# Gate and up projections: seven block products in place of eight, over all tokens at once

## Chip, cores and metric

One core of a Trainium2 chip runs the kernel. The metric is the device time of one execution in microseconds (us), the median of three runs. TensorE is written PE, its weight load PEld, VectorE DVE, ScalarE ACT, GpSimd POOL; SP is the queue that issues most DMAs.

## The reference, cut to what matters

A decoder block over 1024 tokens of width 1024 in float32. What the change touches is the feed-forward part; the first half of the block (a combined input projection, a state-space and a retention group, an output projection) comes ahead of it.

```python
x = x + einsum("bse,ed->bsd", mixed, w_out)
h = rmsnorm(x, norm2_w)
a = silu(einsum("bsd,df->bsf", h, w_gate))     # w_gate: 1024 x 2816
u = einsum("bsd,df->bsf", h, w_up)             # w_up:   1024 x 2816
x = x + einsum("bsf,fd->bsd", a * u, w_down)   # w_down: 2816 x 1024
return rmsnorm(x, final_norm_w)
```

## The kernel before, in words

Every float32 operand of a large projection is split in two: a high part rounded to fp32r (by ACT) and the exact rest (by DVE), `split` at L190 and `divide` at L238. A product of two such operands is three matmuls: high x high, high x low, low x high (`three`, L251).

The tokens are worked on in two halves of 512. A `Block` (L214) is 512 columns of a weight for the tokens of one half. Its steps are the k tiles of the contraction: a step takes a 128-row tile of the weight through 4 output tiles x 3 matmuls of 128x512. All steps of all blocks stand in one list, `steps`, and `run_all` (L316) walks it: at step i it first divides the weights up to step i + 3 (`ahead`, L290), whose loads go out three steps before that on SP's queue (`advance`, L300), then issues the step's matmuls, then what hangs on the step by `at` (L205). Matmuls and transposes keep the order in which they are traced; for the other engines the framework's scheduler picks the order, by priority (weight divisions and evacuations are raised by `PRIO`) and by what is ready.

The order of blocks (L931 to L939) is: input projection of half 0 and of half 1, output projection of half 0 and of half 1, then for each half gate/up (`gate_up_block`, L840) and down (`down_block`, L868). A gate/up block takes 256 gate columns and the 256 up columns that belong to them, 8 steps; there are 11 for each half. Its four sums lie in four of the eight PSUM banks (`banks`, L284); when a sum is complete, `evac` (L850) forms tanh on ACT, multiplies twice on DVE and splits the result into `aT`, 22 pairs of tiles that stay in SBUF (slots m0 to m15, qk, ktok) until the down blocks of the same half have used them. A down block is 22 steps.

The norm ahead of gate/up is `norm_pieces` (L326): `scale` turns the sums of squares into factors and scales four tiles of x in place; eight pieces then transpose 128 channels each through PSUM and split them. The hooks at L1041 to L1048 place half 0's pieces under the output projection of half 1 and half 1's under the down projection of half 0. x after the output projection lies in slots x4 to x7 for half 0 and x0 to x3 for half 1, and is also kept in DRAM (`x2D`), from which the down block loads it again.

Of the kernel before, what the change touches and what calls it, by code (L numbers as in the profile page):

```python
# [29 lines left out]
NXB = 12           # channel tiles of the convolution  # L30

# columns of the constant array
_o = np.cumsum([0, 128, 128, 128, RH * 128, 8 * 32, 8 * 32, RH, RH, 4])
# [3 lines left out]
def _constants():  # L37
    f = np.float32
    c = np.zeros((P, K_N), f)
    i = np.arange(P)  # L40
    c[:, K_ID:K_ID + P] = np.eye(P)
# [16 lines left out]
    return c  # L58
# [6 lines left out]
def block_kernel(ctx: ExitStack, tc: tile.TileContext, x, norm1_w, w_in, conv_w, conv_b,  # L65
# [26 lines left out]
    # ------------------------------------------------------------------ constants  # L92
    kc = T([P, K_N], "kc")
    rows1 = T([8, P], "rows1")
    rows = T([84, P], "rows")
    nc.scalar.dma_start(kc[:, :K_TRI], consts[:, :K_TRI])
# [7 lines left out]
    ident = kc[:, K_ID:K_ID + P]  # L104
# [11 lines left out]
    def load_small():  # L116
        nc.sync.dma_start(kc[:, K_TRI:], consts[:, K_TRI:])
# [9 lines left out]
    # by channel: norm1, norm2, conv_w / 2, conv_b / 2, ret_norm_w / 2, ssd_norm_w  # L127
# [20 lines left out]
    x2D = [[dt_([P, DM], f"x2D{h}{c}") for c in range(NT)] for h in range(2)]  # L148

    # ------------------------------------------------------------------ helpers  # L150
# [5 lines left out]
    def mm(o, a, b, start=True, stop=True):  # L156
        tc.keep_in_program_order(nc.tensor.matmul(o, a, b, start=start, stop=stop))  # L157
# [7 lines left out]
    def rsqrt(dst, src, scale, eps, n):  # L165
        """dst = 1 / sqrt(src * scale + eps), on [P, n]."""
# [11 lines left out]
    def rsqrt1(dst, src, scale, eps):  # L178
        """the same on [P, 1]."""
# [10 lines left out]
    def split(pair, src):  # L190
        """pair[:, 0] = src rounded to fp32r, pair[:, 1] = the exact rest."""
        act(pair[:, 0], src, AF.Copy)
        tt(pair[:, 1], src, pair[:, 0].bitcast(F32), op=ALU.subtract)
# [131 lines left out]
    # ------------------------------------------------------------------ norms  # L325
    def norm_pieces(get, wcol, tags, res):  # L326
        """get() gives NT tiles [P, DM], scaled in place, and their sums of squares; res gets
        the pairs [ch, 2, tok] of what is normed and transposed."""
# [11 lines left out]
        def one(k):  # L340
            def f():
# [3 lines left out]
                hp = T([P, 2, TH], tags[k], F32R)  # L345
# [3 lines left out]
                res.append(hp)  # L349
            return f  # L350
# [89 lines left out]
    def qk_block(h, b):  # L440
        """b=0: dt and q heads 0-3; b=1: q heads 4-7, k heads 0-1; b=2: k heads 2-7."""
# [71 lines left out]
    # ------------------------------------------------------------------ ssd  # L513
# [23 lines left out]
    def cs_stage(h):  # L537
# [11 lines left out]
        ex = T([P, 4, n], "ex", bufs=2)      # a_cs, exp(a_cs), exp(suffix), exp(total)  # L549
# [5 lines left out]
    def hbc(a, c, g, n=SP_):  # L555
        """per head scalars of chunk c, group g, over the n columns of a head."""
# [14 lines left out]
    def ssd_pieces(h, W):  # L571
# [10 lines left out]
        def sz(c, g):  # L582
            def f():
                # 2 * silu(z) by channel; times y in place
# [7 lines left out]
        def s1(c, g):  # L592
            def f():
# [24 lines left out]
                if not first:  # L618
                    C = W([P, 8, P])         # C, decayed from the chunk's start, for each head
# [52 lines left out]
        def s3(c):  # L672
            def f():
                # sums of squares over a group's channels, by token
# [7 lines left out]
        # the first half's z of group 1 comes late  # L682
# [11 lines left out]
    # ------------------------------------------------------------------ retention  # L694
    def ret_pieces(h, W):
# [3 lines left out]
        def r1(c):  # L699
            def f():  # L700
# [9 lines left out]
                # even heads in the first bank, odd heads in the second: their q and k lie on  # L710
                # different halves of the partitions
# [81 lines left out]
    # ------------------------------------------------------------------ out-projection  # L793
    def out_blocks(h):
# [22 lines left out]
                    # the gate carries 2 * silu(z): so does the sum of squares, by 4  # L817
# [15 lines left out]
        # the ssd groups' norms scale their parts of the sum  # L833
# [5 lines left out]
    # ------------------------------------------------------------------ feed-forward  # L839
    def gate_up_block(h, b):  # L840
        d = H[h]

        def begin(blk):
            if b == 0:
                d["aT"] = [T([P, 2, TH], f"m{k}", F32R) for k in range(16)]
                q1 = T([P, 4, 2, TH], "qk", F32R)
                q2 = T([P, 2, 2, TH], "ktok", F32R)
                d["aT"] += [q1[:, k] for k in range(4)] + [q2[:, k] for k in range(2)]

            def evac(j, ps):  # L850
                if j < 2:
                    return
                f = 2 * b + j - 2
                g, u = ps[j - 2], ps[j]
                if j == 2:
                    t = T([P, 2, TH], "S")
                    t, a = t[:, 0, :], t[:, 1, :]
                else:
                    t, a = T([P, TH], "u", bufs=2), T([P, TH], "u", bufs=2)
                act(t, g, AF.Tanh, scale=0.5)  # L860
                stt(t, t, 1.0, g, op0=ALU.add, op1=ALU.mult)
                stt(a, u, 0.5, t, op0=ALU.mult, op1=ALU.mult)
                split(d["aT"][f], a)
            return evac
        return Block(True, lambda: d["hT2"], [(w_gate, 256 * b, 256), (w_up, 256 * b, 256)], begin,
                     pool=None)

    def down_block(h, b):  # L868
        d = H[h]

        def begin(blk):
# [15 lines left out]
            def evac(t, ps):  # L887
# [7 lines left out]
                # the end: no wait but for what the last products give  # L895
# [6 lines left out]
                # the mean square so far, and EPS  # L902
# [3 lines left out]
                if b == 1:  # L906
# [27 lines left out]
    for h in range(2):  # L934
        H[h]["O"] = list(out_blocks(h))
    for h in range(2):
        d = H[h]
        d["GU"] = [gate_up_block(h, b) for b in range(NF // 2)]
        d["D"] = [down_block(h, b) for b in range(2)]  # L939

    # first half's norm
# [66 lines left out]
    def late_small():  # L1008
        # not ahead of the first steps' work, on either engine
# [30 lines left out]

    for h in range(2):  # L1041
        d = H[h]
        d["hT2"] = []
# [38 lines left out]
```

## Time and profile before

| | |
|---|---|
| device time, median of 3 runs | 1579.66 us (1578.94 to 1580.57) |
| profiled execution: span, first to last instruction | 1577.9 us |
| its mean granted PE clock | 0.994 of full speed |
| PE busy | 1555.8 us, 99% |
| DVE busy | 901.3 us, 57% |
| ACT busy | 623.0 us, 39% |
| DMA | 206.65 MB, mean 131 GB/s |

The span is one profiled execution's; that execution's own time is taken as its span and the 1.8 us by which the median of the runs is longer. Busy shares are means over stages that differ. A line number in a row is one of the listing above; L157 is the helper that records every matmul and L160 the one for transposes, so there the tile names tell more: `wp` is a divided weight, `h` a normed activation, `m` a slot of many uses, L and M the two sets of PSUM banks.

### The profile page before, as it was taken

What the parts mean: (1) busy time and instruction counts of PE and PEld (TensorE: products, weight loads), DVE (VectorE), ACT (ScalarE), POOL (GpSimd) and SP (SyncE); (2) the same over time, 40 slices, a digit from 0 to 9 for tenths busy, and PEclk for the clock granted to TensorE, in tenths of its full rate; (3) what the DMA queues carried; (4) which work ended last, traced back from release to release, by engine and by line L of the source; (5) the groups of instructions that cost most, each with busy time, mean ns of one, the idle gap of its engine ahead of it and who ended that gap; (6) DMA issues with size and microseconds to landing.
All of it is one profiled execution on the core that took longest, in us unless ns stands there. A gap on an engine that the chain in (4) does not pass through costs nothing.

```text
span 1577.9 us, 21658 instructions
## 1 busy us (share of the span) xinstructions
PE 1555.8 (99%) x7672; PEld 1272.0 (81%) x7672; DVE 901.3 (57%) x1975; ACT 623.0 (39%) x1195; POOL 36.9 (2%) x67
## 2 busy tenths in 40 slices
PE   7999999999999999999999999999999999999997
PEld 5888878888898888787888888888888888888886
DVE  4477798567798984687544444343326344434244
ACT  5344457435446564244333333232323333323231
POOL 1012000000000000000000000000000000000000
PEclk8999999999999999999999999999999999999999
DMA  7433465554344577466343333333244333332231
GB/s 194 131 90 102 142 199 176 170 183 133 89 114 150 167 236 257 135 197 197 123 154 111 94 93 94 97 95 96 88 147 147 95 93 94 94 93 94 96 110 68
DMA packets 149933, 206.65 MB, mean 131 GB/s; under 512 B 14564, under 2 KB 91200, under 8 KB 149824
## 3 DMA queue, kind: packets, MB, share of 16 engines
q1 hardware_dynamic: 148656, 203.82, 42.2%
q0 software_dynamic: 432, 0.59, 0.6%
q8 instruction: 60, 0.98, 0.3%
q10 hardware_dynamic: 736, 0.86, 0.2%
q14 instruction: 49, 0.40, 0.1%
HBM read 175.78 MB, written 29.43 MB: 130 GB/s over the span
## 4 chain that ended last, share of the span: by engine, by line
PE 97%; DMA 2%; DVE 1%; ACT 1%; issue 0%; SPq 0%; ACTq 0%
PE L L157 77%; PE M L157 18%; PE M L160 2%; DMA wr<-in_w_in_dram 1%; DMA m<-mixD 0%; DMA kc<-in_consts_dram 0%; DMA x2D<-x 0%; DVE x L828 0%; DVE wp L245 0%; ACT x L435 0%; ACT wp L244 0%; ACT m L616 0%; DVE nw L187 0%; ACT u L196 0%; ACT m L806 0%
## 5 line engine op out<-in xcount | busy, mean ns | idle before, releaser
L245 DVE TENSOR_TENSOR wp<-wr,wp 128x512 fp32r<-128x512 f32 (+2 forms) x504 | 339.7, 674 | 571.1 <-ACT wp L244 444.0
L244 ACT ACTIVATE wp<-wr 128x512 fp32r<-128x512 f32 (+2 forms) x504 | 311.7, 619 | 757.5 <-PE L L157 546.2
L157 PE MATMUL L<-h,wp 128*128 128x512 f32 x2280 | 553.5, 396 | 0.0
L157 PEld LDWEIGHTS L<-h,wp 128*128 128x128 f32 x2280 | 425.8, 188 | 103.6 <-issue 1.0
L157 PE MATMUL L<-wp,m 128*128 128x512 f32 x1512 | 357.4, 395 | 0.3 <-DVE x L825 0.3
L157 PEld LDWEIGHTS L<-wp,m 128*128 128x128 f32 x1512 | 282.0, 188 | 65.8 <-DVE x L825 1.0
L157 PE MATMUL L<-wp,h 128*128 128x512 f32 (+2 forms) x1248 | 260.0, 365 | 0.0
L157 PEld LDWEIGHTS L<-wp,h 128*128 128x128 f32 x1248 | 215.3, 188 | 30.6 <-issue 5.1
L157 PE MATMUL M<-h,wp 128*128 128x512 f32 x792 | 198.9, 395 | 0.0
L157 PEld LDWEIGHTS M<-h,wp 128*128 128x128 f32 x792 | 148.5, 188 | 36.1
L378 DVE SCALAR_TENSOR_TENSOR m<-m,cols,m 128x512 f32<-128x512 f32 x72 | 52.1, 745 | 3.6 <-ACT m L376 3.4
L196 ACT ACTIVATE u<-x 128x512 f32<-128x512 f32 x48 | 29.9, 624 | 25.0 <-DVE x L889 19.5
L157 PE MATMUL L<-m,h 128*128 128x512 f32 x96 | 25.9, 421 | 10.7 <-ACT h L984 10.4
L157 PE MATMUL L<-wp,qk 128*128 128x512 f32 x144 | 34.5, 398 | 0.0
L616 ACT ACTIVATE m<-M,dtw 128x64 f32<-128x64 f32 x128 | 29.9, 328 | 11.4 <-DVE m L613 11.3
L806 ACT ACTIVATE m<-m,cols 128x512 fp32r<-128x512 f32 x32 | 22.7, 721 | 27.1 <-DMA m<-mixD 26.8
L157 PEld LDWEIGHTS L<-wp,qk 128*128 128x128 f32 x144 | 27.0, 188 | 6.4
L157 PEld LDWEIGHTS L<-m,h 128*128 128x128 f32 x96 | 18.7, 201 | 16.3 <-ACT h L984 11.7
L157 PE MATMUL M<-m,m 128*64 128x128 f32 (+1 forms) x288 | 30.8, 278 | 0.0
L160 PEld LDWEIGHTS M<-kc,x 128*128 128x128 f32 x192 | 24.3, 145 | 6.8 <-issue 1.8
L160 PE MATMUL M<-kc,x 128*128 128x128 f32 x192 | 29.4, 280 | 0.0
L623 DVE TENSOR_SCALAR m<-m,ex 128x128 f32<-128x128 f32 x128 | 27.9, 279 | 0.1
(213 smaller groups left out, 1163.6 us busy)
## 6 DMA issues: line engine op xcount, KB each, us to landing
wr<-in_w_in_dram SPq DMA_DIRECT2D x144, 256.0 KB, 2.8
wr<-in_w_gate_dram SPq DMA_DIRECT2D x176, 128.0 KB, 2.1
wr<-in_w_up_dram SPq DMA_DIRECT2D x176, 128.0 KB, 2.2
wr<-in_w_down_dram SPq DMA_DIRECT2D x88, 256.0 KB, 2.6
wr<-in_w_out_dram SPq DMA_DIRECT2D x64, 256.0 KB, 3.0
x<-in_x_dram SPq DMA_DIRECT2D x16, 512.0 KB, 4.4
m<-rD SPq DMA_DIRECT2D x16, 512.0 KB, 4.3
m<-mixD SPq DMA_DIRECT2D x32, 256.0 KB, 4.2
```

Of the source, the lines that this page charges most:

```text
L157: tc.keep_in_program_order(nc.tensor.matmul(o, a, b, start=start, stop=stop))
L160: tc.keep_in_program_order(nc.tensor.transpose(o, a, ident))
L196: act(T([P, 512], "u", bufs=2)[:, :src.shape[-1]], src, AF.Square, accum_out=dst)
L244: newest["act"] = act(pair[:, 0, :n], raw[:, :n], AF.Copy).ins
L245: newest["dve"] = tt(pair[:, 1, :n], raw[:, :n], pair[:, 0, :n].bitcast(F32), op=ALU.subtract).ins
L378: stt(dst, u[:, q:q + TH], w[q], dst, op0=ALU.mult, op1=ALU.add)
L616: act(xdte[:, hs], xp[:, hs], AF.Copy, scale=d["dte"][:, r0 + q:r0 + q + 1])
L623: ts(E[:, q, :], E[:, q, :], ex[:, 0, r0 + q:r0 + q + 1], 0.0, op0=ALU.subtract, op1=ALU.min)
L806: act(pair[:, 0], raw, AF.Copy, scale=w)
```

## The change

Gate and up are no longer done for one half of the tokens after the other. A `Unit` is 256 columns of one weight (gate or up) for all 1024 tokens. The weight is cut in four blocks (512 rows of the contraction x 128 columns), the normed activations too (512 channels x 512 tokens), and Strassen's scheme in Winograd's form gives the four blocks of the result by seven block products. A block product is one step: 4 k tiles x 3 matmuls of 128x512. The sums of weight blocks are formed on DVE for each unit (`divide`), the sums of activation blocks once, ahead (`b_first`, `b_sums`, `b_rest`). The products gather in three banks per unit, X, Y and Z; what a bank holds between two products is copied or added out (`c1`, `u2`, `c15`).

The order is now: both output projections, all of gate/up, down of half 0, down of half 1. Since the block sums need both halves normed, half 1's norm follows its output projection at once; the first eight steps of gate/up are products 1 and 2 of the first four units, which need half 0 alone. The other five products of these four units come next, then 18 units of seven. The gated result goes to DRAM (`aD`), and each down projection loads it again and splits it under its first block. Slots change hands: x0 to x3 take the whole weights (1 MB per unit, two loads), x4 to x7 join the divided weights' slots, and the constants' tile is used for sums (the identity moves to a tile of its own). Comments in the code are dropped; lines that only lose a comment are left out of the diff here.

```diff
@@ norm_pieces @@
-    def norm_pieces(get, wcol, tags, res):
+    def norm_pieces(get, wcol, tags, res, also=None):
...
-                hp = T([P, 2, TH], tags[k], F32R)
+                if also and k < 4:
+                    if k == 0:
+                        st["qk"] = T([P, 4, 2, TH], "qk", F32R)
+                    hp = st["qk"][:, k]
+                else:
+                    hp = T([P, 2, TH], tags[k], F32R)
...
                 res.append(hp)
+                if also:
+                    also(k)(b, w)
@@ feed-forward @@
-    def gate_up_block(h, b):
...
+    def b_first(k):
+        def f(b, w):
+            if k < 4:
+                B["F"].append(T([P, 2, TH], f"h{k}" if k < 3 else "S"))
+            act(B["F"][k % 4][:, k // 4, :], b, AF.Copy, scale=w)
+        return f
+
+    def b_sums(k):
+        def f():
...
+            for q in (k + 4, k):
+                b = bank("M")
+                for t in range(NT):
+                    tr(b[:, t * P:(t + 1) * P], H[1]["x2"][t][:, q * P:(q + 1) * P])
+                bs.append(b)
+            t2, t1 = bs
+            b22 = T([P, TH], "u", bufs=2)
+            act(b22, bs[0], AF.Copy, scale=cols[:, 12 + k:13 + k])
+            F = B["F"][k]
+            stt(t1, bs[1], cols[:, 8 + k:9 + k], F[:, 0], op0=ALU.mult, op1=ALU.subtract)
+            tt(t2, b22, t1, op=ALU.subtract)
+            split(B[6][k], t2)
+            split(B[5][k], t1)
+            tt(F, F, t2.unsqueeze(1).to_broadcast([P, 2, TH]), op=ALU.subtract)
+            split(B[3][k], b22)
+        return f
+
+    def b_rest(k):
+        def f():
+            split(B[7][k], B["F"][k][:, 0])
+            B[4].append(T([P, 2, TH], f"h{(k + 3) % 4}", F32R))
+            split(B[4][k], B["F"][k][:, 1])
+        return f
+
+    slots = [("wp", 3), ("x4", 1), ("wp", 3), ("x5", 1), ("wp", 3), ("x6", 1), ("x7", 1)]
...
+    class Unit:
...
+        ORDER = (1, 6, 5, 2, 7, 3, 4)
...
+        def load(self, k):
+            src = self.w[:, self.c0:self.c0 + 256].rearrange("(q k p) c -> q p k c", q=2, p=P)
+            if self.prods == (1, 2):
+                a = T([P, 4, P], "wr", bufs=5)
+                nc.sync.dma_start(a, src[k][:, :, :P])
...
+            elif k == 0:
+                u = self.parity = units[0] % 2
+                units[0] += 1
+                self.raw = [T([P, 4, 256], f"x{2 * u + q}") for q in range(2)]
+                for q in range(2):
+                    nc.sync.dma_start(self.raw[q], src[q])
+
+        def divide(self, k):
...
+                f = {1: A11, 2: A12, 4: A22}.get(i)
+            if i == 6:
+                f, op["s1"] = stage["s2"], T([P, 4, P], "wr", bufs=5)
+                tt(op["s1"], A21, A22, op=ALU.add)
+                tt(f, op["s1"], A11, op=ALU.subtract)
+            elif i == 5:
+                f = op.pop("s1")
+            elif f is None:
+                f = T([P, 4, P], "wr", bufs=5)
+                tt(f, *((A21, A11) if i == 7 else (A12, stage["s2"])), op=ALU.subtract)
+            op[i] = slot()
+            newest["act"], newest["dve"] = split(op[i], f)
+
+        def run(self, k):
+            i, st = self.prods[k], self.st
+            name = "XXYZYZZ"[i - 1]
+            if i in (1, 5, 6):
+                st[name] = next(any_bank)
+            ps, p = st[name], self.op.pop(i)
+            for q in range(4):
+                b = B[i][q]
+                st_ = i in (1, 5, 6) and q == 0
+                mm(ps, p[:, 0, q], b[:, 0, :], st_, False, skip_group_check=True)
+                mm(ps, p[:, 0, q], b[:, 1, :], False, False, skip_group_check=True)
+                mm(ps, p[:, 1, q], b[:, 0, :], False, q == 3, skip_group_check=True)
+            with tc.high_priority(PRIO):
+                if i == 1:
+                    copy(st["c1"], ps)
+                elif i == 6:
+                    st["u2"] = T([P, TH], "RS")
+                    tt(st["u2"], ps, st["c1"], op=ALU.add)
+                elif i == 5:
+                    st["c15"] = stage["c15"][:, self.parity]
+                    tt(st["c15"], ps, st["c1"], op=ALU.add)
+                else:
+                    q, add = {2: (0, None), 7: (3, "c15"), 3: (1, "u2"), 4: (2, "c1")}[i]
+                    self.use(q, ps, st[add] if add else None)
...
+            def gate(q, ps, add):
...
+                    tt(g, ps, add, op=ALU.add)
+                t = temp()
+                act(t, g, AF.Tanh, scale=0.5)
+                stt(ss[q], t, 1.0, g, op0=ALU.add, op1=ALU.mult)
+
+            def up(q, ps, add):
...
+                    tt(u, ps, add, op=ALU.add)
+                a = T([P, TH], "u", bufs=2)
+                stt(a, u, 0.5, ss[q], op0=ALU.mult, op1=ALU.mult)
+                nc.sync.dma_start(aD[q % 2][2 * b + q // 2], a)
...
+        EARLY = 4
+        us += [Unit(*a, (1, 2)) for a in todo[:EARLY]]
+        us += [Unit(*a, (6, 5, 7, 3, 4)) for a in todo[:EARLY]]
+        us += [Unit(*a) for a in todo[EARLY:]]
@@ down_block @@
+        def fetch(k):
...
+            nc.sync.dma_start(a[k][:, 1].bitcast(F32), aD[h][k])
+
+        def extra(k):
+            pair = d["aT"][k]
+            split(pair, pair[:, 1].bitcast(F32))
...
+                     (fetch, extra) if b == 0 else None,
@@ the program @@
+    s0 = H[1]["O"][0].first
+    at(s0 + 5, scale[0])
+    for k in range(8):
+        at(s0 + 9 + 2 * k, ks[0][k])
...
+    s0 = GU[0].first
+    at(s0 - 1, b_ready)
+    at(s0 - 1, scale[1])
+    for k in range(4):
+        at(s0 + 2 + k, b_sums(k))
+        at(s0 + 6, b_rest(k))
...
-    at(H[0]["GU"][2].first, load_final)
+    at(H[0]["D"][0].first, load_final)
```

## Rows read from the trace of the kernel before

**Rows 1.** Page: busy time, share of the span and instructions of each engine

```profile
PE 1555.8 (99%) x7672; PEld 1272.0 (81%) x7672; DVE 901.3 (57%) x1975; ACT 623.0 (39%) x1195; POOL 36.9 (2%) x67
```

**Rows 2.** Page: chain that ended last, shares by engine

```profile
PE 97%; DMA 2%; DVE 1%; ACT 1%; issue 0%; SPq 0%; ACTq 0%
```

**Rows 3.** Chain pieces (start, length, what); a window: engines, clock, DMA share, GB/s

```profile
961.10 23.10 PE L L157 x99
1005.90 23.10 PE L L157 x99
...
961.10:1005.90 44.80, 44.80 (x194) 35.90 (x193) 18.40 (x29) 14.81 (x24) 0.00 (x0) 1.00 0.32 94
```

**Rows 4.** Groups by line and form: busy us, mean ns | idle before

```profile
L245 DVE TENSOR_TENSOR wp<-wr,wp 128x512 fp32r<-128x512 f32 x456 | 315.0, 691 | 547.4 <-ACT wp L244 420.5 <-DMA wr<-in_w_gate_dram 117.4 <-DMA wr<-in_w_down_dram 6.3
L244 ACT ACTIVATE wp<-wr 128x512 fp32r<-128x512 f32 x456 | 288.0, 632 | 718.2 <-PE L L157 517.6 <-PE M L157 158.2 <-issue 32.3
...
L825 DVE SCALAR_TENSOR_TENSOR x<-L,rs,x 128x512 f32<-128x512 f32 x32 | 21.8, 743 | 0.0
...
L621 DVE TENSOR_TENSOR m<-m,m 128x1024 f32<-128x1024 f32 x14 | 17.3, 1234 | 2.2 <-ACT m L620 2.2
...
L860 ACT ACTIVATE S<-L 128x512 f32<-128x512 f32 x22 | 13.2, 600 | 1.5
...
L862 DVE SCALAR_TENSOR_TENSOR u<-M,u 128x512 f32<-128x512 f32 x11 | 7.5, 682 | 0.0
```

**Rows 5.** Timeline, 790 to 836 us: start, length, engine, line

```profile
791.84 0.60 PE L160 MATMUL M<-kc,x 128*128 128x128 f32 x4
...
826.54 23.26 PE L157 MATMUL L<-h,wp 128*128 128x512 f32 x99
...
829.07 0.16 DVE L334 TENSOR_TENSOR rs<-ssq 128x4 f32<-128x4 f32 x1 [0.53 <-ACT u L196]
...
834.17 1.41 DVE L337 TENSOR_SCALAR x<-x,rs 128x1024 f32<-128x1024 f32 x2
```

**Rows 6.** Waits: engine, line <- whom, us in total, times, longest

```profile
ACT m L616 <- DVE m L613: 11.3, 7, 2.8
```

**Rows 7.** DMA issues: kind, count, KB each, median us to landing

```profile
x<-in_x_dram SPq DMA_DIRECT2D x16, 512.0 KB, 4.4
...
m<-mixD SPq DMA_DIRECT2D x32, 256.0 KB, 4.2
...
zD<-x SPq DMA_DIRECT2D x16, 256.0 KB, 3.0
x<-zD SPq DMA_DIRECT2D x16, 256.0 KB, 3.4
```

**Rows 8.** Chain piece before the end, and windows around two idle stretches, as rows 3

```profile
1539.92 28.46 PE L L157 x122
...
1571.50:1572.00 0.50, 0.00 (x0) 0.00 (x0) 0.43 (x3) 0.00 (x0) 0.00 (x0) 1.00 0.00 0
1572.00:1573.00 1.00, 0.00 (x0) 0.00 (x0) 0.85 (x3) 0.61 (x1) 0.00 (x0) 0.50 0.00 0
...
10.00:11.00 1.00, 0.04 (x1) 0.00 (x0) 0.00 (x0) 0.00 (x0) 0.00 (x0) 1.00 0.03 10
...
12.50:13.00 0.50, 0.00 (x0) 0.00 (x0) 0.00 (x0) 0.00 (x0) 0.00 (x0) 0.50 0.76 103
...
24.00:25.00 1.00, 1.00 (x4) 0.77 (x3) 1.00 (x4) 1.00 (x4) 0.00 (x0) 0.50 1.06 422
...
25.50:26.00 0.50, 0.50 (x4) 0.36 (x2) 0.28 (x1) 0.50 (x2) 0.00 (x0) 0.73 0.99 406
```

**Rows 9.** Windows in which DVE is busiest, columns as in rows 3

```profile
220.00:250.00 30.00, 30.00 (x176) 24.22 (x175) 26.81 (x69) 20.30 (x54) 0.00 (x0) 1.00 0.78 245
...
480.00:500.00 20.00, 20.00 (x104) 16.41 (x104) 18.66 (x45) 12.19 (x31) 3.21 (x4) 1.00 0.44 130
...
738.00:760.00 22.00, 21.71 (x95) 17.17 (x94) 18.96 (x34) 9.97 (x16) 0.00 (x0) 1.00 0.55 186
```

More of the change, by code (lines that the diff above doesn't have):

```diff
@@ L57, in _constants @@
         c[64:, K_GC + p] = np.exp(P * lg[2 * p + 1])
-    return c
+    return a
 _CONST = _constants()
@@ L148, in block_kernel @@
     x2D = [[dt_([P, DM], f"x2D{h}{c}") for c in range(NT)] for h in range(2)]
+    aD = [[dt_([P, TH], f"aD{h}{f}") for f in range(NF)] for h in range(2)]
     PRIO = 400
@@ L837, in out_blocks @@
                             (fetch, extra) if b == 0 else None, r0=r0, K=K)
-    def gate_up_block(h, b):
[L841 to L857, printed above, removed]
-                else:
-                    t, a = T([P, TH], "u", bufs=2), T([P, TH], "u", bufs=2)
-                act(t, g, AF.Tanh, scale=0.5)
[L861 to L866, printed above, removed]
+    B = {4: [], 7: [], "F": []}
@@ new lines, in b_rest, with slot, __init__ @@
+    def b_rest(k):
[5 more added lines that the diff above has]
+    slots = [("wp", 3), ("x4", 1), ("wp", 3), ("x5", 1), ("wp", 3), ("x6", 1), ("x7", 1)]
+    nslot = [0]
+    units = [0]
+    stage = {}
+    def slot():
+        tag, n = slots[nslot[0] % 7]
+        nslot[0] += 1
+        return T([P, 2, 4, P], tag, F32R, bufs=n)
+    class Unit:
+        hold = extra = None
+        r0 = 0
+        ORDER = (1, 6, 5, 2, 7, 3, 4)
+        def __init__(self, w, c0, st, use, prods=ORDER):
+            self.w, self.c0, self.st, self.use, self.prods = w, c0, st, use, prods
+            self.first = len(steps)
+            steps.extend((self, k) for k in range(len(prods)))
+            self.last = len(steps) - 1
+            self.K = len(prods)
+            self.op = {}
+        def load(self, k):
[3 more added lines that the diff above has]
+                nc.sync.dma_start(a, src[k][:, :, :P])
+                self.op[self.prods[k], "raw"] = a
+            elif k == 0:
[5 more added lines that the diff above has]
+        def divide(self, k):
+            i, op = self.prods[k], self.op
+            if (i, "raw") in op:
+                f = op.pop((i, "raw"))
+            else:
+                A11, A21, A12, A22 = (self.raw[q][:, :, j * P:(j + 1) * P] for q in range(2)
+                                      for j in range(2))
+                f = {1: A11, 2: A12, 4: A22}.get(i)
[31 more added lines that the diff above has]
+                    tt(st["c15"], ps, st["c1"], op=ALU.add)
+                else:
+                    q, add = {2: (0, None), 7: (3, "c15"), 3: (1, "u2"), 4: (2, "c1")}[i]
+                    self.use(q, ps, st[add] if add else None)
@@ new lines, in gate_up, with temp, c1, pair_of @@
+    def gate_up():
+        def temp():
+            return T([P, TH], "wr", bufs=5)
+        ss = []
+        def c1(n):
+            if n == 0:
+                stage["c1"] = T([P, 4, TH], "ktok")
+                b = T([P, 3, 4, P], "kcB")
+                stage["s2"] = b[:, 2]
+                stage["c15"] = b.rearrange("p k j q -> p k (j q)")
+                a = T([P, 2, TH], "wb0")
+                ss.extend((a[:, 0], a[:, 1]))
+            return stage["c1"][:, n % 4]
+        def pair_of(b):
+            def gate(q, ps, add):
+                if len(ss) == 2 and q:
+                    a = T([P, 2, TH], "S")
+                    ss.extend((a[:, 0], a[:, 1]))
+                g = ps
+                if add is not None:
+                    g = temp()
+                    tt(g, ps, add, op=ALU.add)
+                t = temp()
+                act(t, g, AF.Tanh, scale=0.5)
+                stt(ss[q], t, 1.0, g, op0=ALU.add, op1=ALU.mult)
+            def up(q, ps, add):
+                u = ps
+                if add is not None:
+                    u = temp()
+                    tt(u, ps, add, op=ALU.add)
+                a = T([P, TH], "u", bufs=2)
+                stt(a, u, 0.5, ss[q], op0=ALU.mult, op1=ALU.mult)
+                nc.sync.dma_start(aD[q % 2][2 * b + q // 2], a)
+            return gate, up
+        class St(dict):
+            def __missing__(self, k):
+                assert k == "c1"
+                self[k] = c1(self.n)
+                return self[k]
+        us, todo, n = [], [], 0
+        for b in range(NF // 2):
+            for w, use in zip((w_gate, w_up), pair_of(b)):
+                st = St()
+                st.n = n
+                n += 1
+                todo.append((w, 256 * b, st, use))
+        EARLY = 4
+        us += [Unit(*a, (1, 2)) for a in todo[:EARLY]]
+        us += [Unit(*a, (6, 5, 7, 3, 4)) for a in todo[:EARLY]]
+        us += [Unit(*a) for a in todo[EARLY:]]
+        return us
@@ L868, in down_block @@
     def down_block(h, b):
         d = H[h]
+        def fetch(k):
+            a = d.setdefault("aT", [])
+            if k < 16:
+                a.append(T([P, 2, TH], f"m{k}", F32R))
+            elif k in (16, 20):
+                n = 4 if k == 16 else 2
+                q = T([P, n, 2, TH], "qk" if k == 16 else "ktok", F32R)
+                a += [q[:, j] for j in range(n)]
+            nc.sync.dma_start(a[k][:, 1].bitcast(F32), aD[h][k])
+        def extra(k):
+            pair = d["aT"][k]
+            split(pair, pair[:, 1].bitcast(F32))
@@ L1039, in block_kernel, with b_ready @@
     spread(ret_pieces(1, ring(HT)), H[0]["O"][0].first + 6, H[0]["O"][-1].last - 2)
+    scale, ks = [None] * 2, [None] * 2
+    hT2 = []
     for h in range(2):
[L1042 to L1048 removed]
+        scale[h], ks[h] = norm_pieces(lambda d=H[h]: (d["x2"], d["ssq"]), 8, HT, hT2, b_first)
+    s0 = H[1]["O"][0].first
+    at(s0 + 5, scale[0])
+    for k in range(8):
+        at(s0 + 9 + 2 * k, ks[0][k])
+    def b_ready():
+        B[1], B[2] = hT2[:4], hT2[4:]
+    s0 = GU[0].first
[4 more added lines that the diff above has]
+        at(s0 + 6, b_rest(k))
     def load_final():
```

40 lines of the change are left out of this document (21 added, 19 removed).

## The prediction

> **What bounds the kernel now.** I read the page's busy shares first: PE is busy 1555.8 of 1577.9 us [rows 1]. A busy PE need not be the limit, so the chain that ended last came next: 97% of it is PE [rows 2]. The kernel is a string of matrix products, and a product taken away is time taken away as long as nothing else ends last in its place. The price of one product comes from the gate/up stage. Two chain pieces there start 44.80 us apart [rows 3]; that is two blocks of 96 products of 128x512, so 44.80 / 192 = 233.3 ns each, 2.80 us for a step of 12 (the window's 194 counts those that straddle its edges). In the same window DVE is busy 18.40 us, 41%, ACT 33%, DMA 32%: room is left, though DVE's is what the change spends.
>
> The sum is made against the profiled span of 1577.9 us; the median of the runs, 1579.66, lies 1.8 us above it, work outside the first and last instruction that the change does not touch. I put the differences on the median.
>
> **Products removed.** Before, a block is 4 column tiles x 8 k tiles x 3 products = 96, and 11 blocks for each of two halves make 2112. Put by units of 256 columns of one weight for all 1024 tokens, that is 96 for each of 22. After, a unit has seven block products of 4 k tiles x 3: 84, in all 1848. 264 x 233.3 ns = **-61.6 us**. The products keep form, operand types and 512 columns, so the price holds. The Trainium skill ("TensorE: Matmul & The Clock Gate", Back-to-back issue gap) gives 512/2.4 + 2.5, about 216 ns, for a product of 512 columns; by that the estimate would be -57.0 us. The stage's own rows say 233.3 ns, and I keep them.
>
> **DVE and ACT in the stage.** A full unit now has on DVE: 7 low parts of weights, 4 block sums of weights, 2 partial sums (u2, c15), 3 last sums and 4 multiplications: 20 operations of 128x512. Such operations cost 682 to 691 ns [rows 4], also out of PSUM: 20 x 0.685 = 13.7 us in 7 x 2.80 = 19.6 us, 70%. A unit whose first two products were done early has 17 in 14.0 us: 11.6 us, 83%. ACT has 20 operations of 0.60 to 0.63 us in two units, 12.4 of 39.2 us. Such loads have been borne: DVE at 26.81 of 30 us and 18.66 of 20 us beside a PE without a gap, and 18.96 of 22 beside 0.29 us of idle PE [rows 9]. The tightest place is bank Z: product 7 leaves a sum there that must be read before product 4 adds to it, and only product 3, 2.80 us, lies between; the reading takes 0.69 us and may queue behind two others. I charge **+1 us** for the whole stage, mostly where the 83% units start with a backlog.
>
> **DMA.** Each gate/up weight is read once instead of twice, and the activations go out and come back: 23 MB less, 23 MB more. Stores of 256 KB land in 3.0 us [rows 7]; their two buffers come round after 5.6 us. They stand in SP's queue behind the step that makes them, so the next unit's weights, two loads of 512 KB issued five steps (14 us) ahead, are held back by about a step. They need 4.4 us [rows 7] for the first and, at the 294 GB/s that 94 GB/s at a share of 0.32 stand for [rows 3], 1.8 us more for the second: covered. Without that cover each unit would wait up to 6 us.
>
> **The down projection.** Half 0 now loads its 22 activation tiles and splits them, one per step, as the out projection does with its own: 2 DVE and 2 ACT operations in 2.80 us, under 50%. Their slots come free with products 5, 6, 7 and 3 of the last unit, the first one five steps ahead; 4.2 us to land [rows 7]. The out projection's like stretch lost 0.29 us [rows 9]: **+0.5 us**.
>
> **The seam.** Before, the second half's norm had the whole of the first half's gate/up for cover. Now it and the block sums stand right behind the out projection, with only eight steps (products 1 and 2 of four units, 22.4 us) beside them. Time is counted from the last out-projection product, at 826.5 [rows 5].
> - The norm's scaling starts at +2.6 and ends at +9.1 (835.58) [rows 5]. Three steps cover 8.4: PE waits 0.7.
> - A piece of block sums needs 8 transposes, 1.2 us [rows 5]; the first are through at +10.5. Then in turn: t1 0.74, t2 0.68, high part on ACT 0.63, two low parts 1.38, the double sum 1.23 [rows 4] = 4.7 us, before its banks are free. That readers of one bank take turns I read from ACT waiting for a DVE operation on the same bank [rows 6]. The next piece's last 4 transposes, 0.8 with the handoff, come behind. Into the gaps falls the rest of DVE's work (third low part, weights, evacuations: about 2 us, some 1.4 of it in gaps). So a piece takes 5.5 to 6.3, I take 6.1, where PE needs 2.8 + 1.2 = 4.0.
> - The fourth piece's transposes end at 10.6 + 2 x 6.1 + 4.7 + 0.8 = +28.3; two steps more take PE to +33.9.
> - Only then are x0 to x3 free for the first whole weights: issued +28.4, landed +34.6 (6.2 as above), two block sums and a split, 2.7 us, and handoffs: product 6 starts at +37.6. Undisturbed it would be 8 x 2.8 + 4 x 1.2 = +27.2. Delay **10.4 us**.
> - Product 7 needs b_rest's tiles at +43.2. DVE's work from +10.6 to there is 18.9 (pieces), 4.8 (b_rest up to it), 5.5 (weights), 2.1 (evacuations) = 31.3, so +41.9 without a gap, 1 to 3 us later with: **+0.8**.
> - PE is idle 3.7 us ahead of product 6. At the end of the kernel the granted clock fell from 1.00 (2.4 GHz) to 0.50 (1.2 GHz) 3.6 us after the last product (1568.4 to 1572.0), and at the start within 2.5 us after one at 10.0; it came back some 5.2 us after work resumed at 20.5 [rows 8]. Half of 5.2 us is **+2.6**; with the gap avoided, 0.
>
> The transposes themselves move (32 before and after) and cost nothing new. The copies b_first adds under the out projection are 8 ACT operations of 0.6 us in a stretch where ACT is under half busy [rows 9], and the own tile for the identity is the same load.
>
> Sum: -61.6 + 1 + 0.5 + 10.4 + 0.8 + 2.6 = -46.3: 1579.66 - 46.3 = **1533.4 us**. The seam has no like in the trace. Its lower bound is DVE's bare work, about 6 us (pieces of 5.5, loads found early, no clock loss); its upper bound is all of the DVE work standing alone, +9.1 and 31.3 and 8, about 20 us.
>
> **Rivals.**
> - A short seam: -61.6 + 6 + 0.5 = -55, 1524 to 1528. For it: DVE work is reordered by what is ready. Against: x0 to x3 come free late whatever the order. 0.12.
> - Small waits come back in every unit: DVE at 70 to 83% with evacuations that now sit on the way to the next product on the same bank. At 0.05 to 0.25 us for each of 154 products that is 8 to 38 us: 1541 to 1572. For it: before, a block's banks had a whole block of 22.4 us to be emptied, now one or two steps; against: rows 9. 0.28.
> - Slower: bank Z decides. Product 4 waits for the sum of product 7 behind the weights' work on DVE in each unit; the gain is used up when a unit loses more than 46.3 / 22 = 2.1 us, three DVE operations in the wrong place. At 3 us a unit: 1533 + 66 = 1599. For it: DVE is in order, and a multiplication there waits for ACT's tanh; against: 2.1 us of slack. 0.06.
> - No effect: the products would have to be no fewer, but 84 and 96 can be counted in the code; only losses equal to the gain give this. 0.02.
>
> **How the numbers follow.** The forecast's own case, 1528 to 1541, has 0.52. The range 1522 to 1560 holds it, the short seam and two thirds of the small waits: about 0.8. This kernel's measurement can tell 0.2%, 3.2 us. Faster 0.92, the same 0.02, slower 0.06.
>
> **What would show it.** PE's count lower by 264; two units every 39.2 us in the chain, DVE 27 us of them; a stretch of some 43 us from the last out-projection product to the first product 7, with PE idle in pieces of about 2 us, one of nearly 4 ahead of product 6, and a clock of 0.50 behind that; the down stage as before. Wrong: PE idle in every unit, released by DVE on bank Z or by a weight load; or a seam over 60 us.

## The result, and the profile after

The changed kernel takes 1528.44 us (median of 4, 1527.78 to 1529.71) against 1579.88 us: a ratio of 0.9678, 95% interval 0.9665 to 0.9692, 51.4 us less. The profiled spans say the same, 1577.9 to 1526.7.

First the page of the changed kernel: busy times, what was moved to and from memory, and the shares of the chain that ended last.

```profile
PE 1496.4 (98%) x7408; PEld 1222.3 (80%) x7408; DVE 1018.6 (67%) x2175; ACT 625.2 (41%) x1219; POOL 33.2 (2%) x67
...
HBM read 166.34 MB, written 40.96 MB: 136 GB/s over the span
...
PE 92%; DMA 4%; DVE 2%; ACT 1%; issue 1%; SPq 0%; ACTq 0%; DVEq 0%
```

PE has 264 instructions fewer than in [rows 1], 59.4 us less busy time, and is still most of the chain; about half of the 4% of DMA are loads in the first down block of half 0, below. DVE went from 901 to 1019 us. Reads fell by 9.4 MB and writes rose by 11.5: the weights are read once, the activations go out and come back.

A window of two units, 14 block products, from the middle of the gate/up stage (columns as in [rows 3]):

```profile
1035.57:1074.77 39.20, 39.20 (x170) 31.56 (x169) 25.23 (x41) 11.47 (x21) 0.00 (x0) 1.00 0.25 81
```

168 products in 39.20 us are 233.3 ns each, the price of [rows 3]. PE has no gap; DVE is busy 25.23 us, 64% (27 were forecast), ACT 29%. From product 5 of the first unit, 864.84, to the first down product, 1270.45, there are 145 block products: 145 x 2.80 = 406, and 405.6 passed. **The steady stage loses nothing.**

What is lost lies at two places. The seam, as the timeline of the changed kernel (start, length, engine, line; L163 is the transposes, L886 the operation t1 that opens a piece of block sums, L936 the load of whole weights):

```profile
826.29 2.96 PE L160 MATMUL L<-qk,wp 128*128 128x512 f32 x12
...
829.94 3.05 PE L160 MATMUL L<-h,x 128*128 128x512 f32 x12 [0.69 <-ACT ktok L166]
...
831.45 2.74 DVE L341 TENSOR_SCALAR x<-x,rs 128x1024 f32<-128x1024 f32 x4
...
836.71 0.76 DVE L886 SCALAR_TENSOR_TENSOR M<-M,cols,h 128x512 f32<-128x512 f32 x1 [1.32 <-PE M L163]
...
841.36 0.63 PE L163 MATMUL M<-kc,x 128*128 128x128 f32 x4 [1.38 <-DVE m L196]
...
846.78 0.63 PE L163 MATMUL M<-kc,x 128*128 128x128 f32 x4 [1.55 <-DVE m L196]
...
852.92 0.63 PE L163 MATMUL M<-kc,x 128*128 128x128 f32 x4 [2.26 <-DVE m L196]
...
853.29 0.92 SPq L936 DMA_DIRECT2D x<-in_w_gate_dram  x2
...
853.82 0.75 DVE L886 SCALAR_TENSOR_TENSOR M<-M,cols,S 128x512 f32<-128x512 f32 x1
...
857.00 3.06 PE L160 MATMUL L<-h,wp 128*128 128x512 f32 x12 [0.69 <-ACT ktok L166]
...
861.27 0.74 PE L160 MATMUL L<-m,x 128*128 128x512 f32 x2 [1.20 <-ACT x L195]
...
862.41 2.60 PE L160 MATMUL L<-m,x 128*128 128x512 f32 x10 [0.40 <-DVE x L196]
...
864.84 2.96 PE L160 MATMUL M<-m,wp 128*128 128x512 f32 x12
...
867.64 2.90 PE L160 MATMUL L<-m,x 128*128 128x512 f32 x12
```

The stretch is counted from 826.29, where the first gate/up product starts behind the last of the out projection. Products 2 of the first and of the fourth early unit start 0.69 us late, at 829.94 and 857.00: they wait for ACT to copy out the bank that product 1 has just filled. The scaling (L341) ends at 834.19, +7.9. The second half of each later piece's transposes waits for a bank: 1.38, 1.55, 2.26 us. The four pieces open between 836.71 and 853.82, on average 5.7 us apart. The whole weights are issued at +27.0, product 6 starts at +35.0, product 7 at +41.4.

How much that costs: a run further down (six early units, banks and order) has the like stretch without a wait; there product 6 starts 37.03 us after the last out-projection product, 12 steps of 2.80 and four times 0.86 us for 8 transposes, so up to the end of gate/up PE would need 154 x 2.80 + 4 x 0.86 = 434.6 us. It took 1270.45 - 826.29 = 444.2: **the seam loses 9.5 us**. (The 8.5 that stands in expectations below counts 8 transposes with the forecast's 1.2 us; it is the same seam.) The window from the last out-projection product to product 5 shows who was busy, and one at the end of the longest wait shows the clock:

```profile
826.29:864.84 38.55, 30.38 (x141) 23.26 (x140) 35.49 (x65) 22.89 (x44) 0.00 (x0) 1.00 0.40 123
```

```profile
852.00:853.00 1.00, 0.08 (x1) 0.11 (x2) 1.00 (x3) 0.58 (x1) 0.00 (x0) 1.00 0.00 0
```

DVE is busy 35.49 of 38.55 us, PE 30.38. The granted clock stays at 1.00 although PE has nothing to do for 2.3 us. That is so in this execution; others with the same seam differ, as the last section shows.

The second place is half 0's first down block, from its ninth step on: PE's timeline (with the starts of the next two blocks), and the loads of that stretch (count, KB, median us to landing):

```profile
1270.45 22.69 PE L160 MATMUL L<-wp,m 128*128 128x512 f32 x97
1293.45 3.07 PE L160 MATMUL L<-wp,m 128*128 128x512 f32 x12 [0.30 <-DVE wp L249]
1296.75 5.63 PE L160 MATMUL L<-wp,m 128*128 128x512 f32 x23 [0.24 <-DVE wp L249]
1302.91 0.50 PE L160 MATMUL L<-wp,m 128*128 128x512 f32 x1 [0.52 <-ACT wp L248]
1303.72 6.56 PE L160 MATMUL L<-wp,m 128*128 128x512 f32 x27 [0.31 <-DVE wp L249]
...
1334.45 44.54 PE L160 MATMUL L<-wp,m 128*128 128x512 f32 x192
...
1395.69 44.55 PE L160 MATMUL L<-wp,m 128*128 128x512 f32 x192
```

```profile
m<-aD SPq DMA_DIRECT2D x16, 256.0 KB, 4.6
wr<-in_w_down_dram SPq DMA_DIRECT2D x15, 256.0 KB, 4.5
x<-x2D SPq DMA_DIRECT2D x6, 512.0 KB, 6.0
```

PE waits 0.30, 0.24, 0.52 and 0.31 us, 1.4 us together, for the divided weights. The loss is larger than these waits: this block takes 64.00 us, the next, with as many products, 61.24. So **2.8 us** are lost, and the 1.4 of the expectations below is only the recorded part. Loads of 256 KB land in 4.5 to 4.6 us there; the kernel before had 2.6 us for such weights over its whole length, and the 4.2 of [rows 7] for tiles of this kind.

So: 264 x 0.2333 = 61.6 less, 9.5 and 2.8 more, 49.3 less in all; the spans differ by 51.2. The other 1.9 us belong to no term: 1.1 lie behind the start of the last products (11.1 us to the end before, 10.0 after), 0.3 ahead of gate/up, and the 32 transposes took 3.9 us in half 0's down projection before and 3.4 in the seam now.

### The profile page after: what moved, and what is told of

It reads as the page before. It is cut to its first block, busy times and chain, and to the rows that moved or that the text cites. A ratio compares the mean times of both kernels' runs of the same rounds, so it can differ in the third digit from the quotient of the medians.

```text
span 1526.7 us, 20790 instructions
## 1 busy us (share of the span) xinstructions
PE 1496.4 (98%) x7408; PEld 1222.3 (80%) x7408; DVE 1018.6 (67%) x2175; ACT 625.2 (41%) x1219; POOL 33.2 (2%) x67
## 4 chain that ended last, share of the span: by engine, by line
PE 92%; DMA 4%; DVE 2%; ACT 1%; issue 1%; SPq 0%; ACTq 0%; DVEq 0%
PE L L160 74%; PE M L160 16%; PE M L163 2%; DMA m<-aD 1%; DMA wr<-in_w_in_dram 1%; DMA wr<-in_w_down_dram 1%; DVE m L196 0%; DMA x<-in_w_gate_dram 0%; DMA kc<-in_consts_dram 0%; DMA ktok<-aD 0%; ACT m L195 0%; DMA m<-mixD 0%; DVE wp L249 0%; DVE u L1019 0%; ACT wp L248 0%
## 5 line engine op out<-in xcount | busy, mean ns | idle before, releaser
L249 DVE TENSOR_TENSOR wp<-wr,wp 128x512 fp32r<-128x512 f32 (+2 forms) x328 | 217.7, 665 | 224.3 <-ACT wp L248 223.1
L248 ACT ACTIVATE wp<-wr 128x512 fp32r<-128x512 f32 (+2 forms) x328 | 199.6, 610 | 361.8 <-PE L L160 294.9
L160 PE MATMUL L<-h,wp 128*128 128x512 f32 x972 | 234.1, 398 | 0.7 <-ACT ktok L166 0.7
L160 PEld LDWEIGHTS L<-h,wp 128*128 128x128 f32 x972 | 180.6, 188 | 44.5 <-ACT ktok L166 1.1
L160 PE MATMUL L<-m,x 128*128 128x512 f32 x336 | 82.7, 395 | 1.6 <-ACT x L195 1.2
L160 PE MATMUL L<-h,x 128*128 128x512 f32 x336 | 83.3, 396 | 0.7 <-ACT ktok L166 0.7
L160 PE MATMUL L<-m,wp 128*128 128x512 f32 x312 | 77.1, 395 | 0.0
L160 PEld LDWEIGHTS L<-m,x 128*128 128x128 f32 x336 | 62.9, 188 | 17.2 <-ACT x L195 1.6
L160 PEld LDWEIGHTS L<-h,x 128*128 128x128 f32 x336 | 62.9, 188 | 16.3 <-ACT ktok L166 1.1
L160 PEld LDWEIGHTS L<-m,wp 128*128 128x128 f32 x312 | 58.5, 187 | 14.4
```

Of the source, the lines that this page charges most:

```text
L248: newest["act"] = act(pair[:, 0, :n], raw[:, :n], AF.Copy).ins
L249: newest["dve"] = tt(pair[:, 1, :n], raw[:, :n], pair[:, 0, :n].bitcast(F32), op=ALU.subtract).ins
```

## Experiments

Line numbers in diffs are left out; each edit is made to the changed kernel unless it says otherwise.

### What a block product is worth, and the bank between two of them

```diff
-            for q in range(4):
+            for q in range(0 if i == 2 and self.K == 7 else 4):
```

> The matmuls of block product 2 are left out in the 18 full units (the evacuation stays), so that the sums lack that part. Theory (PE alone ends last in the steady stage): 18 x 2.80 = 50.4 us less than the changed kernel, 1478 us, with DVE at 13.7 of 16.8 us, 82%, and no wait of PE inside a unit. Rival (DVE, ACT or bank turnover is close behind): under 40 us less, 1488 us or more, with PE idle in every unit.

Measured: 1477.63 us, 50.8 less. A window of 100 us from its steady stage:

```profile
1000.00:1100.00 100.00, 100.00 (x430) 80.50 (x429) 75.37 (x120) 34.50 (x60) 0.00 (x0) 1.00 0.30 95
```

PE has no gap with DVE at 75%: one block product less in seven was simply 2.80 us less. By the 216 ns of the Trainium skill ("TensorE: Matmul & The Clock Gate", Back-to-back issue gap), which are its figure for an isolated product of 512 columns, the 216 products left out would be an estimated 46.7 us; the measured 50.8 are 235 ns each, and the trace's own price stands. That the total comes so near to 50.4 is in part luck: in this run's trace the seam takes 3.4 us more than in the changed kernel, and half 0's first down block 2.8 less.

The same with `i == 3`:

> The matmuls of block product 3 are left out in the 18 full units (the evacuation stays), so that product 4 follows product 7 on bank Z at once. Theory of the Z bank rival: PE now waits for the sum of product 7 to be read, at least 0.7 us for one DVE operation and up to 2 us with others ahead of it, in each of 18 units: 50.4 - (13 to 36) us less, 1491 to 1514 us. If the bank's turnover were free, 1478 us as with product 2.

Measured: 1496.82 us, 31.6 less instead of 50.4. Waits of PE in that run:

```profile
PE L L160 <- DVE wr L1017: 6.0, 7, 1.3
...
PE M L160 <- DVE wr L1008: 3.9, 5, 0.8
PE L L160 <- DVE wr L1008: 3.1, 4, 0.8
PE M L160 <- DVE wr L1017: 1.6, 2, 0.8
```

and two of them in PE's timeline:

```profile
952.66 3.06 PE L160 MATMUL L<-h,x 128*128 128x512 f32 x12 [0.78 <-DVE wr L1017]
...
970.51 1.67 PE L160 MATMUL L<-h,x 128*128 128x512 f32 x6 [0.78 <-DVE wr L1008]
```

With nothing between products 7 and 4, PE waits in all 18 units for the operation (L1008 in gate, L1017 in up) that reads bank Z. Recorded as idle are 14.6 us, 0.78 us each and 1.27 for the last, but from one wait to the next 17.85 us pass where six products of 2.80 take 16.80: a stop costs 1.05 us, and 18 of them are the 18.8 us that are missing. The rival of bank Z is a real mechanism, but one block product between the two uses covers it, and in the changed kernel it costs nothing.

```diff
-            for q in range(4):
+            for q in (0, 1, 2, 3, 0, 1, 2, 3) if i == 3 else range(4):
```

> The matmuls of block product 3 are issued twice in all 22 units, which makes eight block products, as many matmuls as the kernel before (the sums then hold that part twice). Theory (264 matmuls at 233.3 ns are the gain, the rest of the change costs 8.5 us at the seam and 1.4 us at the start of the down projection): 61.6 us more, 1590 us, some 10 us above the kernel before. Rival (part of the gain comes from elsewhere, such as the weights read once): close to or under the kernel before, 1580 us.

Measured: 1587.87 us, ratio to the kernel before 1.0054, interval 1.0038 to 1.007. With as many products as before, the new structure is slower than the old one by 8 us: the gain is the count of products. It is 59.4 us above the changed kernel, 2.2 short of 61.6: in the traces the stretch from the first gate/up product to the first down product is 62.4 us longer, and half 0's first down block, which loses nothing in this run, 2.8 us shorter.

### The way through memory alone

The kernel before with the stores of `aD` and the `fetch` and `extra` of the changed `down_block`:

```diff
-                split(d["aT"][f], a)
+                nc.sync.dma_start(aD[h][f], a)
...
+                     (fetch, extra) if b == 0 else None,
```

> The kernel before with one part of the change alone: the gated activations go through DRAM, and each down projection loads and splits them under its first block. Theory: the round trip hides, at most 1.5 us at each of two starts of a down projection where loads crowd: 1580 to 1583 us. Rival: each start waits for a store to land and a load to land, 3.0 + 4.2 us twice: 1594 us.

Measured: 1578.39 us, ratio 0.9991 (0.9981 to 1.0). There is no wait of PE at either start of a down projection, and 0.7 us of what the run gained had been gained before the first instruction that the edit touches. The round trip costs nothing by itself.

### What sets the seam's end

```diff
-        EARLY = 4
+        EARLY = 3
```

> Three units instead of four have their products 1 and 2 ahead of the block sums, 5.6 us less cover. Theory (the chain of DVE operations from the scaled x to product 7 sets the seam's end, whatever PE has beside it): the sums end earlier only by the 2 us of DVE work that goes with the fourth early unit, so 3 to 5.6 us more than the changed kernel, 1531 to 1534 us. Rival (PE's waits come from what the early steps themselves bring, their copies and banks): under 1 us more.

Measured: 1533.11 us, 4.7 more. PE ran out of work, and then worked slowly (PE's timeline):

```profile
852.77 0.63 PE L163 MATMUL M<-kc,x 128*128 128x128 f32 x4 [1.51 <-DVE m L196]
861.45 5.10 PE L160 MATMUL L<-m,x 128*128 128x512 f32 x12 [8.05 <-ACT x L195]
```

Product 6 starts 8.05 us after the last transposes, at 34.8 us from the last out-projection product (35.0 in the changed kernel): its start is set by what is behind the sums. It also takes 5.10 us where 2.96 are usual, at a granted clock of 0.50 (from 855.4 to 865.7).

```diff
-                b = bank("M")
+                b = bank("M" if q == k + 4 else "L")
```

> The second bank of each piece of block sums comes from the other set (L), so that no transposes wait for a bank that an earlier piece still reads. Theory (DVE's work ends last): the waits of 5.2 us ahead of transposes vanish from PE but come back ahead of products 6 and 7, the time falls by at most 1.5 us, 1527 to 1529 us. Rival (the turnover of the banks ends last): 4 to 5 us less, 1523 to 1525 us.

Measured: 1528.44 us, no change. PE's timeline:

```profile
848.41 0.60 PE L163 MATMUL L<-kc,x 128*128 128x128 f32 x4
...
857.04 0.74 PE L160 MATMUL L<-m,x 128*128 128x512 f32 x2 [1.52 <-ACT x L195]
...
862.95 0.50 PE L160 MATMUL L<-m,x 128*128 128x512 f32 x1 [2.88 <-ACT m L195]
864.12 0.83 PE L160 MATMUL L<-m,x 128*128 128x512 f32 x2 [0.67 <-DVE m L196]
864.75 4.44 PE L160 MATMUL M<-m,wp 128*128 128x512 f32 x12
```

All transposes are through at 848.8, +21.4 instead of +27.1, and the whole weights come that much earlier, but product 6, begun at 857.04, stops for the split activation blocks (2.88 and 0.67 us), and the clock falls:

```profile
865.00:867.00 2.00, 2.00 (x6) 1.52 (x6) 2.00 (x3) 0.16 (x1) 0.00 (x0) 0.50 0.00 0
```

The waits moved, as the theory had it. Product 6 follows the last transposes at a nearly fixed distance: 8.4 us from their start in the changed kernel (852.92 to 861.27), 8.7 with three early units, 8.6 here. In that time the whole weights land, some 5 us, and are summed and split.

```diff
+    def split_pool(pair, src):
+        act(pair[:, 0], src, AF.Copy)
+        nc.gpsimd.tensor_tensor(pair[:, 1], src, pair[:, 0].bitcast(F32), op=ALU.subtract)
...
-            split(B[3][k], b22)
+            split_pool(B[3][k], b22)
...
-            split(B[4][k], B["F"][k][:, 1])
+            split_pool(B[4][k], B["F"][k][:, 1])
```

> The low parts of the activation blocks of products 3 and 4 (eight operations of 128x512 that read only SBUF) go from DVE to POOL. Theory (DVE's work ends last): 4.8 us of DVE work (seven operations of 0.69) leave the stretch ahead of product 7, the seam shrinks by 2.5 to 4.8 us, 1524 to 1526 us. Rival (whole weights or banks end last, or POOL's slower operations, about 1.9 us each by the 1.41 us for 128x384 in the kernel before, come too late): less than 1 us.

Measured: 1527.51 us (1523.9 to 1529.3), 0.9 less, within its spread; a miss. The window of the seam, from the last out-projection product to product 5:

```profile
824.97:862.72 37.75, 30.38 (x142) 23.26 (x140) 31.94 (x58) 22.52 (x44) 9.45 (x7) 1.00 0.40 125
```

DVE's work fell by 3.55 us, from 35.49 to 31.94, but the stretch only from 38.55 to 37.75. (The trace is of an execution of 1523.9 us. Of the 4.6 us by which its span is shorter than the changed kernel's, 1.3 lie ahead of gate/up and 2.4 in half 0's first down block, which the edit does not touch.) So DVE's sum of work is not all that ends last. The banks' turnover and the loads that wait for the last transposes make a second chain of nearly the same length; as this run and the one before it show, taking either away leaves the other.

```diff
-        EARLY = 4
+        EARLY = 6
-    slots = [("wp", 3), ("x4", 1), ("wp", 3), ("x5", 1), ("wp", 3), ("x6", 1), ("x7", 1)]
+    slots = [("wp", 3), ("x4", 1), ("wp", 3), ("x5", 1), ("wp", 3), ("x6", 1)]
-        return stage["c1"][:, n % 4]
+        return stage["c1"][:, n % 6] if n % 6 < 4 else stage["c1b"][:, n % 6 - 4]
```

> Six units instead of four have products 1 and 2 ahead of the block sums (the two further copies take the slot x7, which leaves the ring of divided weights). Theory: 11.2 us more of products lie beside the sums and bring about 4 us of DVE work, so the seam's 8.5 us fall to 1 to 3 us: 1520 to 1523 us. Rival (the sums wait for PE's order of transposes and early steps rather than the other way round): no change, 1528 us.

Measured: 1531.01 us, 2.6 more: a miss, and not by the rival's reason alone. PE's waits, and a window behind the last transposes:

```profile
PE M L163 <- DVE m L196: 6.2, 3, 2.4
PE L L160 <- ACT ktok L166: 1.4, 2, 0.7
...
PE L L160 <- ACT x L166: 0.8, 1, 0.8
...
PE M L160 <- ACT x L166: 0.7, 1, 0.7
```

```profile
858.00:859.00 1.00, 1.00 (x3) 0.73 (x3) 1.00 (x3) 0.00 (x0) 0.00 (x0) 0.50 1.09 383
```

Product 6 now waits for nothing. But the cover itself is full of holes: 6.2 us for banks, 2.9 for the copies (four instead of two), and a clock of 0.50 from 855.8 to 859.2, under which one step took 4.59 us. They add up to some 11 us, a little more than the seam had cost.

### Closing the seam

Only the order of the early steps:

```diff
         us += [Unit(*a, (1, 2)) for a in todo[:EARLY]]
+        for u in range(0, EARLY, 2):
+            i = us[u].first
+            steps[i + 1], steps[i + 2] = steps[i + 2], steps[i + 1]
```

> Only the order of the eight early steps is changed: products 1 of two units, then products 2 of the two, so that no product 2 waits for ACT's copy of the bank that product 1 has just filled. Theory (DVE's chain ends last): the two waits of 0.7 us vanish and come back ahead of product 6, 1527.5 to 1529 us. Rival (waits of PE add up): 1.4 us less, 1527 us.

Measured: 1529.02 us (1526.94 to 1529.85), no change: the waits for copies are gone and PE waits 3.1 us ahead of product 6 instead.

The three together:

> Six early units, the second bank of each piece of block sums from set L, and the early steps in pairwise order, together. In the run with six early units alone the sums ended in time for product 6, but PE had waited 6.2 us for banks and 2.9 us for copies, with the clock at 0.50 for some 4 us. Theory (both sides are needed: cover for DVE's chain, and no wait inside the cover): these go, the seam's 8.5 us fall to 1 to 3, 1521 to 1523 us. Rival (the bank waits only move, as they did with four early units): 1527 to 1530 us.

Measured: 1517.20 us, ratio to the kernel before 0.9608 (0.9593 to 0.9622), 11.2 less than the changed kernel; in the traces 10.0 of this lie between the first gate/up product and the first down product, 1.1 in half 0's first down block. Its window behind the last out-projection product at 826.35:

```profile
826.00:870.00 44.00, 44.00 (x208) 36.00 (x207) 40.87 (x74) 27.13 (x52) 0.00 (x0) 1.00 0.47 144
```

PE 44.00 of 44 us at full clock, DVE 40.87. None of the three had helped alone. Whether banks or order matter more once there are six early units was not tried.

### The start of the down projection

```diff
                 for t in range(NT):
-                    nc.sync.dma_start(d["x3"][t], x2D[h][t])
+                    at(blk.first + 13 + t, lambda t=t: ld(t))
...
-    at(H[0]["D"][0].first, load_final)
+    at(H[0]["D"][0].last, load_final)
```

> The down blocks load their four tiles of x (2 MB) under steps 13 to 16 of their first block instead of ahead of it, and the final norm's weights come at the end of half 0's first block. Theory (the 1.4 us that PE lost late in half 0's first down block come from loads that crowd at the start of the down projection): they vanish, 1526.5 to 1527.5 us. Rival (it is the pair of loads per step, 512 KB in 2.80 us, that is too much): no change.

Measured: 1527.21 us (1526.03 to 1527.72), 1.2 less. The window that answers to the stretch with the waits:

```profile
1290.00:1303.70 13.70, 13.70 (x60) 11.08 (x59) 5.82 (x10) 5.14 (x9) 0.00 (x0) 1.00 0.80 287
```

No gap of PE is left there, and the block takes 61.25 us. That the edit did it is not shown. The waits come and go from run to run where the down projection is as in the changed kernel: the block loses nothing in the traces of product 2 left out and of product 3 twice, and 0.3 us in that of the low parts on POOL. And they are back in the next run, which loads x late as well. Six early units, banks, order, POOL and late loads together:

> Six early units, banks from both sets, pairwise order, the low parts of the blocks of products 3 and 4 on POOL, and the late loads of x and of the final norm's weights, together. Theory: the seam's 8.5 and the down projection's 1.4 us nearly vanish, 1519 to 1522 us. Rival (POOL's operations come late for product 3, or slow DVE's): slower than the run before last, over 1523 us.

Measured: **1516.03 us, ratio 0.9601 (0.9587 to 0.9616)**, the fastest of all, 12.4 under the changed kernel; over the run with three edits it is 1.2 us, which the ranges do not separate. The seam is closed here too, but half 0's first down block takes 63.45 us, 2.2 more than the second, and PE waits in it for divided weights as before:

```profile
1275.54 11.14 PE L160 MATMUL L<-wp,m 128*128 128x512 f32 x47 [0.30 <-DVE wp L253]
1287.36 0.50 PE L160 MATMUL L<-wp,m 128*128 128x512 f32 x1 [0.68 <-ACT wp L252]
```

So late loads did not keep these waits away here, and what sets them stays open.

## Why the prediction was right, and by how much its terms were off

Forecast 1533.4 us, 46.3 less; measured 1528.4, 51.4 less, inside the range of 1522 to 1560 and on the faster side. The mechanism was the one forecast; that the sum came within 5 us is in part luck, since the terms missed in both directions and 1.9 us of the gain lie in none of them.

- **Products removed, -61.6.** Right. Two ways to vary the count gave 235 ns (one product out) and 225 ns (one twice; 235 with the 2.8 us of the down block put back) for one matmul; the steady window gave 233.3.
- **DVE and ACT in the stage, +1.** Measured 0. DVE was at 64% where 70% was forecast, because operations that follow each other start 0.60 us apart though each is recorded with 0.69: a sum of means counts the overlap twice. Two block sums of weights from the timeline of the changed kernel:

```profile
858.65 0.69 DVE L948 TENSOR_TENSOR wr<-x,x 128x512 f32<-128x512 f32 x1 [0.49 <-DMA x<-in_w_gate_dram]
859.26 0.69 DVE L954 TENSOR_TENSOR wr<-x 128x512 f32<-128x512 f32 x1
```

- **DMA, 0.** Right; the loads of whole weights were never waited for in the steady stage.
- **Down projection, +0.5.** Measured 2.8 in the trace of the changed kernel, and 0 to 2.6 in those of the later runs; not at the start as the slots come free, but eight to twelve steps on, when loads land late. Which of the loads (weights, activations, x) puts the others behind is not shown. The lone round trip in the kernel before costs nothing.
- **Seam, +13.8.** Measured 9.5. This is the term that was mis-sized. Step by step: the scaling ended at +7.9, not +9.1, since fewer weight divisions stood between; pieces came 5.7 us apart, inside the 5.5 to 6.3 given but under the 6.1 taken; the whole weights were issued at +27.0 (forecast +28.4), and landed in about 5 us (6.2); product 6 started at +35.0 (+37.6) and product 7 at +41.4 (+44.0). The early steps ended at +33.8 (forecast +33.9), so that PE stood only 1.2 us ahead of product 6 instead of 3.7, and the **+2.6 for the clock did not come** in this execution: the granted clock stayed at 1.00. That was luck as well, for in four other traces with the same seam it fell to 0.50 for a stretch (last section); in the run with late loads, whose waits up to the fall are the same, the way from the first gate/up product to the first down product is 1.4 us longer. Against that, the wait of two second products for ACT's copy, 2 x 0.69 us, was not in the sum, and 8 transposes, priced 1.2 us by their records, take 0.86.
- The forecast had the loads behind the last transposes set product 6, and DVE's work product 7. The expectations of the later runs had DVE's chain alone end last; that was too simple. The experiments show two chains, the banks with the loads behind them and DVE's work, within about 1 us of each other.
- **Rivals.** The short seam was given 6 us and came to 9.5, between it and the forecast. Small waits in every unit: none. Bank Z: 1.05 us a unit when product 3 does not lie between, nothing as it is. No effect: with eight products the time is 8 us above the kernel before, so the count makes the gain.

## What to carry to other kernels

With PE as the chain and DVE at 41% in the stage, trading products for sums paid the full price of the products here, as long as no bank is used again in the very next product. The cost then sits where the new operands are made: look for what must be finished before the first product that needs them, and count bank turnover, copies and loads each as a chain of its own. If closing one hole changes nothing, close them together before giving up: three edits that did nothing or harm one by one took the seam away jointly.

## What the runs showed of the hardware that was not expected

- The clock's fall does not follow from the waits alone. In the changed kernel it stayed at 1.00 through waits of 1.38, 1.55 and 2.26 us between bursts. In the run with late loads, whose seam is the same code, the waits up to there were 1.39, 1.56 and 2.26 us, and it fell to 0.50, so that the next step's record grew from 2.96 to 4.59 us:

```profile
852.33 0.73 PE L163 MATMUL M<-kc,x 128*128 128x128 f32 x4 [2.26 <-DVE m L196]
852.71 4.59 PE L160 MATMUL L<-qk,x 128*128 128x512 f32 x12
```

```profile
853.00:856.00 3.00, 3.00 (x9) 2.33 (x8) 3.00 (x6) 1.75 (x3) 0.00 (x0) 0.50 0.71 186
```

  The run with product 3 left out shows the same fall behind the same waits. Those with product 2 left out and product 3 twice fell only later, with waits of 3.10 and 2.19 us ahead of product 6. With three early units and 8.05 us of idle it fell as well.
- A stop of PE costs more than its recorded idle: 1.05 us for 0.78 at bank Z, time after time.
- POOL did the low part of a 128x512 block in 1.27 to 1.75 us, against the 0.68 to 0.69 us of DVE and the 1.9 that the expectation had scaled from a 128x384 operation.
- Four transposes in a row take 0.43 to 0.44 us of PE from start to start when nothing waits (848.0 to 848.4 with banks from both sets); the 0.60 us of [rows 5] is the length of their record.
